# A short store of zeros into the output, issued beside the first load of a streaming softmax

## The chip, the cores and the metric

One core of one Trainium2 chip runs the kernel. The metric is the time of one execution on the device in microseconds (us), lower is better. Nine executions of the kernel before, taken in one series, lie between 317.75 and 318.42 us (0.2%), so an effect of half a microsecond in 318 needs several runs and the trace to be seen.

## The reference

A softmax over the last axis with a temperature of 0.5; the input is 32 x 512 rows of 1024 float32 values, 64 MB in and 64 MB out.

```python
def reference(x, temperature):
    scaled = x / temperature
    shifted = scaled - np.max(scaled, axis=-1, keepdims=True)
    exp_x = np.exp(shifted)
    return (exp_x / np.sum(exp_x, axis=-1, keepdims=True)).astype(np.float32)
```

## The kernel before

Sixteen tiles of 4 MB (128 partitions x 8 rows of 1024) stream through six buffers. SyncE (SP) issues the loads and ScalarE (ACT) the stores. VectorE (DVE) takes maxima over groups of four rows and divides; ScalarE exponentiates. Each partition's 8 rows lie next to each other in memory, so a load or a store is 128 pieces of 32 KB.

```python
TILES = [[8]] * 16
BUFS = 6
GROUP = 4
# ... pools, groups, dram() cut
    def load():
        i = len(tiles)
        if i < len(TILES):
            xt = data.tile([P, sum(TILES[i]), d], f32, name="xt")
            nc.sync.dma_start(out=xt, in_=dram(xf, i))                   # L61
            tiles.append(xt)
# ... maximum, exponential, divide cut: L70, L79, L91 and L93 of the profile
    def store(g):
        i, _, _, part = groups[g]
        if part:
            a, k = part
            nc.scalar.dma_start(out=dram(of, i)[:, a : a + k, :],
                                in_=tiles[i][:, a : a + k, :])           # L101
            if a + k == sum(TILES[i]):
                load()

    with tc.manual_schedule():
        for _ in range(BUFS):
            load()
        for g in range(len(groups) + 1):
            if g < len(groups):
                maximum(g)
                exponential(g)
            if g > 0:
                divide(g - 1)
                store(g - 1)
```

Of the kernel before, what the change touches and what calls it, by code (L numbers as in the profile page):

```python
# [1 line left out]

# [4 lines left out]
# [9 lines that stand above are left out]
@with_exitstack  # L16
def kernel(
    ctx: ExitStack,
    tc: tile.TileContext,
    x: bass.AP,  # L20
    temperature: bass.AP,
    out: bass.AP,
):
    nc = tc.nc
    f32 = mybir.dt.float32
    scale = 1.0 / float(temperature)
    extreme = mybir.AluOpType.max if scale > 0 else mybir.AluOpType.min

    P = 128
    xf = x.flatten_outer_dims()  # L30
    of = out.flatten_outer_dims()
    n, d = xf.shape
    assert sum(sum(ks) for ks in TILES) * P == n

    data = ctx.enter_context(tc.tile_pool(name="data", bufs=BUFS))
    stats = ctx.enter_context(tc.tile_pool(name="stats", bufs=4))


    groups, first, r = [], [], 0
    for i, ks in enumerate(TILES):  # L40
        first.append(r)
        r += sum(ks)
        a = 0
        for k in ks:
            for b in range(0, k, GROUP):
                m = min(GROUP, k - b)
                groups.append((i, a + b, m, (a, k) if b + m == k else None))
            a += k

    def dram(t, i):  # L50
        k = sum(TILES[i])
        block = t[P * first[i] : P * (first[i] + k), :]
        return block.rearrange("(p k) d -> p k d", p=P, k=k)

    tiles, small = [], []
# [8 lines that stand above are left out]
    def maximum(g):  # L64
        i, a, k, _ = groups[g]
        top, bias, sums, recip = (
            stats.tile([P, k], f32, name=name) for name in ("top", "bias", "sums", "recip")
        )
        small.append((bias, sums, recip))
        nc.vector.tensor_reduce(  # L70
            out=top, in_=tiles[i][:, a : a + k, :], axis=mybir.AxisListType.X, op=extreme
        )
        nc.vector.tensor_scalar_mul(bias, in0=top, scalar1=-scale)  # L73

    def exponential(g):
        i, a, k, _ = groups[g]
        bias, sums, _ = small[g]
        for b in range(k):
            nc.scalar.activation(  # L79
                tiles[i][:, a + b, :],  # L80
                tiles[i][:, a + b, :],
                mybir.ActivationFunctionType.Exp,
                bias=bias[:, b : b + 1],
                scale=scale,
                accum_out=sums[:, b : b + 1],
            )

    def divide(g):
        i, a, k, _ = groups[g]
        _, sums, recip = small[g]  # L90
        nc.vector.reciprocal(recip, sums)  # L91
        for b in range(k):
            nc.vector.tensor_scalar_mul(  # L93
                tiles[i][:, a + b, :], in0=tiles[i][:, a + b, :], scalar1=recip[:, b : b + 1]
# [6 lines that stand above are left out]
            nc.scalar.dma_start(out=dram(of, i)[:, a : a + k, :], in_=tiles[i][:, a : a + k, :])  # L101
            if a + k == sum(TILES[i]):
                load()



    with tc.manual_schedule():
        for _ in range(BUFS):
            load()
        for g in range(len(groups) + 1):  # L110
# [8 lines that stand above are left out]
# [1 line left out]
_INS = ['x', 'temperature']  # L120
_OUTS = [((32, 512, 1024), 'float32')]

_NUMBERS = {'temperature': 0.5}


# [26 lines left out]
```

## Time and profile before

| before | |
|---|---|
| time, median of 3 runs | 317.91 us (317.78 to 318.01) |
| span of the profiled run | 316.0 us |
| data packets | 4096 of 32 KB, 256 per DMA engine, median 1.213 us each: 310.5 us |
| first data packet starts / last packet ends | 1.74 us / 314.80 us |
| VectorE busy | 75% |

The packet rows come from the trace's record of every DMA packet (start, duration, bytes, queue). Sixteen engines at 32768 bytes per 1.213 us make 432 GB/s. From 1.74 us to the end they hardly ever stop, so the kernel is bound by DMA, and any microsecond that all engines lose should reach the end.

From the profile page of the kernel before: busy times, the DMA row over 40 slices of 7.9 us (9 is 90% or more busy), the two queues (q1 is SyncE's, with the loads; q10 is ScalarE's, with the stores: packets, MB, share of 16 engines), and the chain of work that ended last.

```profile
span 316.0 us, 620 instructions
...
DVE 235.5 (75%) x224; ACT 149.6 (47%) x257; POOL 0.2 (0%) x4
...
DMA  8999999999999999999999999999999999999996
...
DMA packets 4612, 134.25 MB, mean 425 GB/s; under 512 B 512, under 2 KB 512, under 8 KB 512
...
q1 hardware_dynamic: 2304, 67.11, 49.7%
q10 hardware_dynamic: 2304, 67.11, 49.2%
...
DVE 49%; DMA 32%; another core or an unknown queue 9%; ACT 5%; issue 1%; DVEq 0%; SPq 0%
```

The reader should see the nines in the DMA row and the shares of the queues: 49.7% and 49.2% add up to 99%. The chain names VectorE for half of the span, but it is no steady measure: it names VectorE for 49% here and for 72% in the trace of the memset alone (below), which runs equally fast. An engine that is busy 75% does not bound a kernel whose DMA engines are busy 99%.

From the timeline of the kernel before, its start and its last stores (start, duration, both in us, engine, line, operation; in brackets, how long the engine had been idle and what released it). "SPq" and "ACTq" are DMA issues, x6 means six merged.

```profile
0.73 2.91 SPq L61 DMA_DIRECT2D xt<-in_x_dram  x6
12.96 4.42 DVE L70 TENSOR_REDUCE top<-xt 128x4 f32<-128x4096 f32 x1 [12.96 <-DMA xt<-in_x_dram]
13.01 1.28 ACT L79 ACT_TABLE_LOAD   x1 [13.01 <-DMA xt<-in_x_dram]
...
32.66 0.37 ACTq L101 DMA_DIRECT2D out_dram<-xt  x1
...
302.38 0.34 ACTq L101 DMA_DIRECT2D out_dram<-xt  x1
```

VectorE and ScalarE idle for 13 us, the first store is issued at 32.66 us and the last at 302.38.

Beyond the 310.5 us, the packet records hold two groups of load packets that take longer than 1.213 us. I call "stretch" the sum of what the load packets took beyond 1.213 us, divided by 16 engines:

```
kernel before, load packets over 1.26 us          packets   durations          stretch per engine
1.74 to 2.10 us   (first packet of each engine)        16    1.66 to 2.06 us    0.69 us
33.93 to 35.92 us (after the first store's issue)      28    1.27 to 2.60 us    0.81 us
rest of the kernel                                      4    1.48 to 1.75 us    0.14 us with smaller ones
```

The second group begins 1.27 us after the first store is issued. This group is what the change could hope to remove. In the table of windows (DVE, ACT, POOL busy, TensorE clock, DMA share, GB/s) it shows only coarsely, because a window of 4 us holds about three packets per engine and each is counted at once:

```profile
30.00:33.00 3.00, 3.00 (x5) 3.00 (x5) 0.00 (x0) 1.00 1.14 492
33.00:37.00 4.00, 3.97 (x2) 1.45 (x4) 0.00 (x0) 1.00 0.87 287
```

### The profile page before, as it was taken

To read this page: it belongs to the slowest core of one execution; us is meant where nothing else is said; L and a number is where in the kernel's file an instruction comes from. 1 tells how busy PE (TensorE), PEld (TensorE's weight loads), DVE (VectorE), ACT (ScalarE), POOL (GpSimd) and SP (SyncE) were. 2 spreads that over 40 slices of the span, in tenths; PEclk is the share of its full clock that TensorE was granted. 3 is DMA by queue.
4 is the path that set the end of the run, shared out by engine and by line. 5 is a ranking of instruction groups with operands and counts; after the bars stand their busy time and mean duration, and the time that the engine had idled before them with its cause. 6 is when DMAs were issued, how large, how long until landed. Compare 5 with 4: busy or idle time off the path is not lost.

```text
span 316.0 us, 620 instructions
## 1 busy us (share of the span) xinstructions
DVE 235.5 (75%) x224; ACT 149.6 (47%) x257; POOL 0.2 (0%) x4
## 2 busy tenths in 40 slices
DVE  0399999999689494994949859497693976949720
ACT  0176666666526255361554605546064560645500
POOL 0000000000000000000000000000000000000000
DMA  8999999999999999999999999999999999999996
GB/s 332 411 452 423 373 460 415 452 425 431 436 427 440 427 444 423 444 419 448 415 452 411 452 408 456 423 444 427 436 431 432 440 423 444 419 444 419 452 411 274
DMA packets 4612, 134.25 MB, mean 425 GB/s; under 512 B 512, under 2 KB 512, under 8 KB 512
## 3 DMA queue, kind: packets, MB, share of 16 engines
q1 hardware_dynamic: 2304, 67.11, 49.7%
q10 hardware_dynamic: 2304, 67.11, 49.2%
q14 instruction: 4, 0.03, 0.0%
HBM read 67.11 MB, written 67.11 MB: 425 GB/s over the span
## 4 chain that ended last, share of the span: by engine, by line
DVE 49%; DMA 32%; another core or an unknown queue 9%; ACT 5%; issue 1%; DVEq 0%; SPq 0%
DVE top L70 29%; DMA xt<-in_x_dram 20%; DVE xt L93 18%; DMA out_dram<-xt 12%; ACT xt L79 5%; DVE recip L91 1%; DVE bias L73 1%; DVEq L147 0%; SPq L61 0%
## 5 line engine op out<-in xcount | busy, mean ns | idle before, releaser
L79 ACT ACTIVATE xt<-xt,bias 128x1024 f32<-128x1024 f32 x128 | 145.4, 1137 | 136.8 <-DVE recip L91 119.4
L70 DVE TENSOR_REDUCE top<-xt 128x4 f32<-128x4096 f32 x32 | 141.3, 4416 | 62.6 <-DMA xt<-in_x_dram 62.6
L93 DVE TENSOR_SCALAR xt<-xt,recip 128x1024 f32<-128x1024 f32 x128 | 87.7, 749 | 1.1
L79 ACT ACTIVATION_READ_ACCUMULATOR xt<-xt,bias 128x1 f32 x128 | 23.9, 187 | 0.0
L79 ACT ACT_TABLE_LOAD x1 | 1.3, 1283 | 13.0 <-DMA xt<-in_x_dram 13.0
L91 DVE RECIPROCAL recip<-sums 128x4 f32<-128x4 f32 x32 | 5.5, 171 | 2.1 <-ACT xt L79 2.1
L73 DVE TENSOR_SCALAR bias<-top 128x4 f32<-128x4 f32 x32 | 5.4, 170 | 1.1
L133 POOL MEMSET const-bfloat16-1.0<- 128x1 bf16 x1 | 0.1, 101 | 0.0
L133 POOL MEMSET const-uint8-127<- 128x1 uint8 x1 | 0.1, 101 | 0.0
L133 POOL MEMSET const-float32-0.0<- 128x1 f32 x1 | 0.1, 98 | 0.2 <-issue 0.2
L133 POOL MEMSET const-float32-1.0<- 128x1 f32 x1 | 0.1, 98 | 0.0
## 6 DMA issues: line engine op xcount, KB each, us to landing
xt<-in_x_dram SPq DMA_DIRECT2D x16, 4096.0 KB, 50.2
out_dram<-xt ACTq DMA_DIRECT2D x16, 4096.0 KB, 38.6
```

The costliest lines, as they stand in the source:

```text
L70: nc.vector.tensor_reduce(out=top, in_=tiles[i][:, a : a + k, :], axis=mybir.AxisListType.X, op=extreme)
L73: nc.vector.tensor_scalar_mul(bias, in0=top, scalar1=-scale)
L79: nc.scalar.activation(tiles[i][:, a + b, :], tiles[i][:, a + b, :], mybir.ActivationFunctionType.Exp, bias=bias[:, b : b + 1], scale=scal ...
L91: nc.vector.reciprocal(recip, sums)
L93: nc.vector.tensor_scalar_mul(tiles[i][:, a + b, :], in0=tiles[i][:, a + b, :], scalar1=recip[:, b : b + 1])
L133: nc = _bacc.Bacc("TRN2", target_bir_lowering=False, num_devices=1)
```

## The change

A tile of 128 x 128 zeros is cleared on VectorE and stored from ScalarE's queue into the first 512 bytes of each partition's share of the first output tile, before anything else. The first tile's real store overwrites it. The likely intent is to use the store queue and the output once while nothing depends on them.

```diff
+    zeros = stats.tile([P, 128], f32, name="zeros", bufs=1)
     with tc.manual_schedule():
+        nc.vector.memset(zeros, 0.0)
+        nc.scalar.dma_start(out=dram(of, 0)[:, 0, :128], in_=zeros)
         for _ in range(BUFS):
             load()
```

## The prediction

> **What bounds the kernel now.** The DMA engines. The page's DMA row is 9 in 38 of 40 slices, 425 GB/s over the span, for 134 MB. The trace's records of single DMA packets say it more sharply: 4096 data packets of 32 KB, 256 on each of 16 engines, median 1.213 us. That is 432 GB/s in all, close to the 435.2 GB/s fabric ceiling that the Trainium skill gives (DMA: Bandwidth & Descriptors, section "Where 436 GB/s comes from"). 256 x 1.213 = 310.6 us of the 316.0 us span. The first packet starts at 1.74 us, the last one ends at 314.8; over these 313.1 us the engines lie idle 1.6 us on average, nearly all in the last microsecond. VectorE is busy 75% and waits 62.6 us for loads (list of waits); it does not bound the whole.
>
> The rest above 310.6 us is a few stretched packets, in two clusters. (1) The first packet on each engine takes 1.66 to 2.06 us: about 0.7 us lost once. (2) Right after the first store is issued (32.66 us), two load packets in a row on each engine stretch, to about 1.5 and 1.8 us: about 0.8 us lost by all 16 engines, once. No later store shows it. In the table of windows, 33 to 37 us moves 287 GB/s (coarse: a packet is counted at once).
>
> **What the change does.** Adds a memset of 128x128 on VectorE (estimated 0.1 to 0.2 us, from 0.75 us for a 128x1024 operation), while VectorE waits for the first load until 12.96 us anyway: free. Adds one DMA issue on ScalarE's queue (0.34 us, as the others there), also in idle time. Adds 128 packets of 512 B, 64 KB: 0.15 us at 432 GB/s; with per-packet overhead I estimate 0.2 to 0.4 us, partly inside the latency of the first load's packets. The order of instructions shows that DMA semaphores shift by one: the sixth load now waits for the first load (13 us), which costs nothing, as four loads are still queued then; the first tile's store waits for the zeros, landed about 28 us before. All else keeps its order.
>
> **What it may gain.** ScalarE's queue and the output are now used first at about 1 to 2 us. If cluster (2) is a cost of first use of that queue (or of the first write), it is paid there, overlapping cluster (1), and the 0.8 us at 34 to 37 us go. All DMA time is on the critical path: load 15 lands at 281 us, computing it ends just as store 14 drains, and store 15 follows without a gap; an early gain reaches the end whole. Net: -0.8 x 0.7 (my trust in the mechanism) + 0.2 = about -0.4 us, rounded to -0.5.
>
> **Prediction.** 317.4 us, 8 in 10 between 316.9 and 318.3. Chances: faster by over 2% 0.01, within 2% 0.97, slower by over 2% 0.02. A gain of 2%, 6.4 us, is more than all idle and stretched time found.
>
> **What would show it.** The zeros' packets between 1.5 and 4 us; no packet over 1.3 us between 33 and 37 us; the first load landing at most 0.4 us later than now (12.2 us after its issue); later loads landing and the last store issued about 0.5 us earlier.
>
> **What would make it wrong.** The stretched packets come from the first large store itself (its descriptors, or the turn from reading to writing under load), and stay: then 318.1 us. Or the two slow starts add up: 318.0. Or short writes cost far more than their bytes.

## The result

| | before | after |
|---|---|---|
| time, median of 6 runs | 318.01 us (317.78 to 318.39) | 318.46 us (318.18 to 319.06) |
| ratio | | 1.0017 (95%: 1.0004 to 1.003) |
| span of the profiled run | 315.99 us | 316.40 us |
| last DMA packet ends | 314.80 us | 315.00 us |
| from there to the end of the span | 1.19 us | 1.41 us |
| stretch after the first real store | 0.81 us | 0.70 us |

Ratios are the mean time of one kernel's fast runs over that of the other's of the same rounds, so they are not quite the ratio of the medians. By the medians the kernel became slower by about half a microsecond (the interval of the ratio allows 0.1 to 1.0), where I had predicted it faster by as much; 318.46 lies above the range that ended at 318.3.

From the profile page after; the chain is now told as mostly DMA, which says nothing new, as the chain is unsteady (see above):

```profile
span 316.4 us, 623 instructions
...
DVE 235.6 (74%) x225; ACT 149.6 (47%) x257; POOL 0.2 (0%) x4
...
DMA  8999999999999999999999999999999999999995
...
DMA packets 4756, 134.32 MB, mean 425 GB/s; under 512 B 528, under 2 KB 656, under 8 KB 656
...
q1 hardware_dynamic: 2304, 67.11, 49.6%
q10 hardware_dynamic: 2448, 67.18, 49.2%
...
DMA 57%; DVE 26%; ACT 6%; another core or an unknown queue 4%; issue 1%; DVEq 0%; SPq 0%
```

The store queue has 144 packets more: 128 of zeros and 16 that signal completion. From the timeline after:

```profile
0.73 12.70 SPq L61 DMA_DIRECT2D xt<-in_x_dram  x6
0.82 0.17 DVE L111 MEMSET zeros<- 128x128 f32 x1 [0.82 <-PEq L138]
1.02 0.41 ACTq L112 DMA_DIRECT2D out_dram<-zeros  x1
13.11 4.42 DVE L70 TENSOR_REDUCE top<-xt 128x4 f32<-128x4096 f32 x1 [12.12 <-DMA xt<-in_x_dram]
13.16 1.28 ACT L79 ACT_TABLE_LOAD   x1 [13.16 <-DMA xt<-in_x_dram]
...
32.81 0.34 ACTq L101 DMA_DIRECT2D out_dram<-xt  x1
...
302.54 0.34 ACTq L101 DMA_DIRECT2D out_dram<-xt  x1
```

The memset takes 0.17 us and delays nothing. The six load issues now stretch over 12.70 us instead of 2.91, because the sixth waits for the first load; that is the shift of semaphores foreseen. It costs nothing: the sixth load's last packet ends at 86.57 us (86.44 before). In this pair of traces VectorE starts 0.15 us later, the first and the last real store are issued 0.15 and 0.16 us later, and the last packet ends 0.20 us later. That looks like one early delay carried to the end, but single traces scatter as much: with the memset alone (below) VectorE starts at 12.94 us, yet the last store is issued 0.12 us later than before and the last packet ends at 314.94 us. What an early packet costs at the end is measured by the eightfold store below.

From the list of DMA issues after (KB each, median us from issue to landing):

```profile
out_dram<-zeros ACTq DMA_DIRECT2D x1, 64.0 KB, 14.5
```

64 KB needed 14.5 us to land. The packet records show why. On one engine, in the kernel after:

```
start us   duration   bytes   queue
 6.088      27 ns       512   q10 (zeros)
 6.111    1213 ns     32768   q1  (load)
 7.321      27 ns       512   q10
 7.344    1213 ns     32768   q1
 8.553      27 ns       512   q10
```

The engine takes one packet from each queue in turn. That is what the Trainium skill says (DMA: Bandwidth & Descriptors, section "Queues, rings and completion order": each engine goes round the queue rows it has work for, packet by packet), and the trace agrees, if one record of it is taken as a packet: 8 packets of zeros per engine lie between 6.09 and 14.02 us, one per load packet. Each costs the engine 27 ns, so the store costs every engine 8 x 27 ns = 0.22 us. The turns do not explain why the first packet starts only 5.07 us after the issue at 1.02 us, for a turn lasts 1.24 us. The first real store behaves likewise: issued at 32.81 us, its first packet starts at 37.20 us. What fills this time is not shown.

From the same windows after:

```profile
30.00:33.00 3.00, 2.97 (x5) 3.00 (x5) 0.00 (x0) 1.00 0.91 393
33.00:37.00 4.00, 4.00 (x1) 1.59 (x4) 0.00 (x0) 1.00 1.01 360
```

One might read 360 against 287 GB/s as a gain. It is not: the window before it lost as much, as packets moved across the edge. The records of single packets show load packets stretched from 34.12 us on, 1.31 us after the first real store's issue, by 0.70 us per engine in all. The zeros did not remove them.

The last 0.2 us come after all data has landed. The records of the queue instructions at the end of the program, which no view lists, show ScalarE late at its last DRAIN (the trace's name for an instruction with which each engine closes the program):

```
last DRAIN of            SyncE starts    ScalarE starts, takes     span ends
before                     315.56          315.57      8 ns         315.99
after                      315.77          316.05    136 ns         316.40
```

Each engine's last record follows only after all have been at this point (ScalarE's starts at 315.93 us before, 316.34 after). Before, ScalarE is there with SyncE; after, 0.28 us later.

So the theory was: 0.22 us for the zeros' packets, about 0.2 us for a late end of ScalarE's instruction stream, and no gain, because the stretch does not come from first use of the queue or of the output.

### The profile page after: what moved, and what is told of

The parts are those of the page before. It is cut to its first block, busy times and chain, and to the rows that moved or that the text cites. A ratio compares the mean times of both kernels' runs of the same rounds, so it can differ in the third digit from the quotient of the medians.

```text
span 316.4 us, 623 instructions
## 1 busy us (share of the span) xinstructions
DVE 235.6 (74%) x225; ACT 149.6 (47%) x257; POOL 0.2 (0%) x4
## 4 chain that ended last, share of the span: by engine, by line
DMA 57%; DVE 26%; ACT 6%; another core or an unknown queue 4%; issue 1%; DVEq 0%; SPq 0%
DMA xt<-in_x_dram 35%; DMA out_dram<-xt 22%; DVE top L70 17%; DVE xt L93 9%; ACT xt L79 6%; DVE recip L91 1%; DVE bias L73 0%; DVEq L152 0%; SPq L61 0%
## 6 DMA issues: line engine op xcount, KB each, us to landing
out_dram<-zeros ACTq DMA_DIRECT2D x1, 64.0 KB, 14.5
```

## The experiments

"Stretch" is as above, over the 6 us after the issue named. "Tail" is the time from the last packet's end to the end of the span. All runs were correct. Those with five rounds are compared with runs of the kernel before on the same chip.

### The change once more

No edit.

> The change itself once more, for its size on the same chip as the three below. Theory A (the zeros' own packets cost the DMA engines 8 x 27 ns each, about 0.2 us, and the ScalarE instruction stream, one DMA longer, loses another 0.2 us in the teardown after the last packet, as in the first trace, where ScalarE's last DRAIN came 0.28 us after the other engines' and took 136 ns): 0.3 to 0.6 us slower than before. Theory B (the second three of the six runs, 319.0, were only scatter, and the real cost is the packets alone): 0.1 to 0.3 us slower. In the trace: stretched load packets at 34 to 37 us again, summing to 0.7 to 0.8 us per engine.

Measured: 318.45 us against 317.94, ratio 1.0013 (1.0 to 1.0025), tail 1.38 us, ScalarE's last DRAIN 0.29 us behind SyncE's and 136 ns long; stretch after the first real store 0.52 us. The slowdown of half a microsecond is there again, though the interval begins at 1.0; the two runs at 319.0 of the first series did not come again and are taken as scatter. The stretch fell below the 0.7 expected, but it is there, on 19 packets.

### The memset alone

```diff
-        nc.scalar.dma_start(out=dram(of, 0)[:, 0, :128], in_=zeros)
```

> The memset stays, the store goes. Both theories: equal to before within 0.1 us, for the memset runs while VectorE waits for the first load. If it is slower by 0.2 us or more, the cost is not in the DMA at all. Stretched packets at 34 to 37 us as before.

Measured: 317.98 against 317.94, ratio 1.0 (0.9987 to 1.0012), tail 1.19 us, stretch 0.94 us. The memset is free. Over the traces in which the first real store is issued near 33 us (leaving out that with the early 16-partition store), the stretch is 0.70 to 0.94 us in the six without zeros on ScalarE's queue and 0.52 to 0.75 us in the four with them. A saving of about 0.1 us by the zeros can't be told from scatter, nor excluded; one of the whole 0.8 us is excluded.

### The zeros on the other queue

```diff
-        nc.scalar.dma_start(out=dram(of, 0)[:, 0, :128], in_=zeros)
-        for _ in range(BUFS):
+        load()
+        nc.sync.dma_start(out=dram(of, 0)[:, 0, :128], in_=zeros)
+        for _ in range(BUFS - 1):
             load()
```

> The same zeros store, but issued on SyncE's queue right after the first load; ScalarE's instruction stream and queue are as before. Theory A: 0.1 to 0.3 us slower than before (packets only), and in the trace 0.75 us instead of 0.95 us between the last store's landing seen by SyncE and the end of the span. If the cost comes from the use of ScalarE's queue as such: no cost. The zeros land near 13 us, right behind the first load. The stretch at 34 to 37 us stays at 0.7 to 0.8 us, as ScalarE's queue is now used first by the first real store.

Measured: 318.22 against 317.94, ratio 1.0005 (0.9993 to 1.0018), tail 1.21 us, no late DRAIN, stretch 0.80 us. From the list of DMA issues:

```profile
out_dram<-zeros SPq DMA_DIRECT2D x1, 64.0 KB, 12.1
```

The medians differ by 0.28 us, as expected for the packets alone, though the interval includes zero. The tail is back at its old value, and that is read from the trace, not from the times.

### The store eight times as large

```diff
-    zeros = stats.tile([P, 128], f32, name="zeros", bufs=1)
+    zeros = stats.tile([P, 1024], f32, name="zeros", bufs=1)
-        nc.scalar.dma_start(out=dram(of, 0)[:, 0, :128], in_=zeros)
+        nc.scalar.dma_start(out=dram(of, 0)[:, 0, :], in_=zeros)
```

> The store is 8 times as large (4 KB per partition, 512 KB in all), the same 8 packets per engine. If early DMA time reaches the end one for one: 8 x 4 KB at 27 GB/s is 1.21 us per engine, so 1.2 to 1.7 us slower than before. If the change's cost is a fixed one (an extra DMA, a longer stream, a shifted semaphore): 0.4 to 0.6 us slower, as the change itself. If a larger early store primes what the first real store stretches on, the stretch at 34 to 37 us shrinks below 0.4 us per engine and the time is 0.4 us lower than that.

Measured: 319.31 against 317.94, ratio 1.0041 (1.0027 to 1.0055), so 1.37 us slower. The zeros' 8 packets per engine took 159 ns each, 1.27 us together, against 0.22 us in the change: 1.05 us more, and the kernel is 0.86 us slower than the change in the medians and 1.21 us in the spans. So DMA time lost in the first microseconds reached the end about one for one. The tail is 1.41 us, the stretch 0.75 us: a larger early store does not remove it either.

### The last store moved off ScalarE's queue

On top of the change:

```diff
-            nc.scalar.dma_start(out=dram(of, i)[:, a : a + k, :], ...)
+            queue = nc.sync if i == len(TILES) - 1 else nc.scalar
+            queue.dma_start(out=dram(of, i)[:, a : a + k, :], ...)
```

> The change, with the last tile's store issued from SyncE instead of ScalarE: ScalarE has again 16 DMA issues, as before the change, while the zeros stay on ScalarE's queue. Theory S (ScalarE's longer instruction stream, 321 recorded instructions against 319 and 320, makes its last DRAIN late): from the last packet's end to the end of the span about 1.2 us as before, not 1.4; time 0.1 to 0.3 us above before, about 0.2 below the change. Theory Q (having used ScalarE's queue for a short store is what costs in the teardown): 1.4 us, 0.4 to 0.5 above before.

Measured: 318.09 against 317.94, ratio 1.0009 (0.9995 to 1.0023), tail 1.21 us, no late DRAIN. The zeros are still stored from ScalarE, but ScalarE's stream is down to 320 recorded instructions and the 0.2 us are gone. Use of the queue is not the reason for the tail.

### ScalarE's stream made longer without any store

Kernel before, with two or with 24 tiny copies:

```diff
+    tiny = stats.tile([P, 2], f32, name="tiny", bufs=1)
     with tc.manual_schedule():
+        nc.vector.memset(tiny, 0.0)
+        for _ in range(2):      # 24 in the other kernel
+            nc.scalar.copy(out=tiny[:, 1:2], in_=tiny[:, 0:1])
```

> The kernel before, with no store of zeros, but two tiny copies (128x1) ahead of ScalarE's work, so that its stream is as long as the change's. Theory S: 1.4 us from the last packet to the end, ScalarE's last DRAIN of 136 ns 0.2 to 0.3 us behind the other engines', and 0.15 to 0.25 us slower than before, with no extra DMA at all. Theory Q: 1.2 us and equal to before within 0.1 us.

> The same with 24 tiny copies (about 5 us of ScalarE's idle time before 13 us). If Theory S is about where the end of ScalarE's stream falls (a fixed spot in it where an instruction comes late), 24 instructions more move that spot away from the end, into time in which ScalarE waits: 1.2 us from the last packet to the end, equal to before within 0.1 us. If any longer stream is slower: 1.4 us, 0.15 to 0.25 us slower, as with two.

Measured with two copies: 318.15 against 317.94, ratio 1.001 (0.9997 to 1.0022), tail 1.39 us, ScalarE's last DRAIN 0.27 us late and 135 ns long. With 24: 318.10, ratio 1.0009 (0.9996 to 1.0021), tail 1.17 us, no late DRAIN; its five times scatter from 317.79 to 318.56, so the expectation of equal times within 0.1 us was not met, while that of the tail was. Put together, from the traces:

```
recorded ScalarE instructions   kernels                                      last DRAIN late   tail
319                             before, memset alone,                        no                1.19, 1.19,
                                the three with a store held back (below)                       1.15, 1.16, 1.19
320                             zeros on the other queue, last store moved,  no                1.21, 1.21, 1.20
                                the early 16-partition store (below)
321                             the change (twice), 8 times as large,        0.27 to 0.29 us   1.41, 1.38, 1.41,
                                two tiny copies                                                1.39
322                             the early whole-tile store (below)           no                1.30
343                             24 tiny copies                               no                1.17
```

The late end goes with one length of the stream and not with the zeros. Two tiny copies, without any extra DMA, produce it.

The DMA records hold a sign of why. The queue of instructions (q14) carries 8 KB packets, and three of them move when ScalarE's stream grows: with 24 copies they start at 49.23, 162.32 and 279.08 us, for about 65.0, 181.93 and 316.96 us before. The third lies near the end of the program in most kernels: 1.03 to 1.41 us after ScalarE's last DRAIN starts where the stream has 319 or 320 instructions, 0.65 to 0.93 us after it where it has 321, and before it where it has 322 (at 325.62 us, DRAIN at 332.98) or 343. So the late DRAIN stands next to a fetch of instructions. That the fetch delays it is not shown.

### When does the stretch come: the second store held back

Kernel before; the second tile's store is issued with the third's, so that the store queue runs empty for a while.

```diff
+                if g - 1 == 3:
+                    continue
+                if g - 1 == 5:
+                    store(3)
                 store(g - 1)
```

> The kernel before, with the second tile's store held back and issued together with the third's (near 62 us instead of 47), so that ScalarE's queue runs empty from about 56 to 62 us while loads go on. Theory R (load packets stretch whenever 32 KB store packets join after the store queue was empty): a second group of stretched load packets from about 63 to 67 us, again 0.5 to 0.9 us per engine, beside the one at 34 to 37 us. Theory F (it is paid once, by the first large store of the kernel): no more than the 0.1 to 0.2 us that the records already show there beside an instruction fetch at 65 us.

Measured, one run: 322.84 us. The first store was issued at 32.63 us, with a stretch of 0.80 us. The next issue found the queue without data packets since 54.48 us:

```profile
59.90 0.34 ACTq L101 DMA_DIRECT2D out_dram<-xt  x1
...
62.19 0.34 ACTq L101 DMA_DIRECT2D out_dram<-xt  x1
```

Up to 65 us no load packet stretched at all; two did then, beside an instruction fetch, as in the kernel before. These stores joined again after a pause and did not pay; the theory that they must falls, on one run. The 4.9 us that this kernel lost came later (see the last section).

### The first store later

Kernel before; in the first kernel the first tile's store is held back until the second's, in the other by half a tile.

```diff
+                if g - 1 == 1:
+                    continue
+                if g - 1 == 3:      # 2 in the other kernel
+                    store(1)
                 store(g - 1)
```

> The kernel before, with the first tile's store held back and issued with the second's, near 47.4 us. Theory F: the stretched load packets move with the issue, to about 48.5 to 52 us, 0.5 us or more, none at 33 to 37.5 us. Theory P: none at 33 to 37.5 us, and little (under 0.3 us) at 48.5 to 52 us, as the load then stands in the middle of its tile. Theory T (something else at this time, not the store): 0.7 us stays at 33 to 37.5 us.

> The same with the first store one half-tile later (near 40 us instead of 32.7). Theory F: stretch of 0.5 us or more from about 41 to 45 us. Theory P: under 0.3 us there, and then perhaps 0.3 to 0.7 us faster than before, unless the later start of the stores costs as in the run with the second store held back.

Measured: 318.27 us (one run) and 318.72 us against 318.01, ratio 1.0033 (1.0011 to 1.0054). From the timeline with the store held until the second's, and of the half-tile kernel in the second block:

```profile
44.93 0.37 ACTq L101 DMA_DIRECT2D out_dram<-xt  x1
...
47.52 0.34 ACTq L101 DMA_DIRECT2D out_dram<-xt  x1
```

```profile
37.19 0.37 ACTq L101 DMA_DIRECT2D out_dram<-xt  x1
...
47.41 0.34 ACTq L101 DMA_DIRECT2D out_dram<-xt  x1
```

Both issues came earlier than I had said (44.9 for 47.4, 37.2 for 40), as a held store waits for nothing. The stretched load packets came from 46.17 us (0.76 us per engine) and from 38.80 us (1.02 us); neither kernel shows any between 33 us and its own first store. So the stretch follows the first store, wherever the load then stands in its tile, and holding it back gains nothing.

### One early store of full-size packets, 16 partitions

Kernel before:

```diff
                 exponential(g)
+                if g == 0:
+                    nc.scalar.dma_start(out=dram(of, len(TILES) - 1)[0:16],
+                                        in_=tiles[1][0:16])
```

> The kernel before, with one early store of full-size packets: 16 partitions x 32 KB of the second tile, raw, to rows that the last tile's store overwrites, issued from ScalarE near 22.3 us, one packet per engine. Theory F (the stretch of 0.7 to 0.8 us is paid once, by the first store with large packets): the stretched load packets move to about 23.5 to 27 us, and 33 to 37.5 us shows under 0.2 us; time 1.2 us (the 16 extra packets) above before. Theory P (the stretch comes from where in its tile a load stands when the first whole-tile store joins, whatever was stored before): 0.5 us or more stays at 33 to 37.5 us.

Measured: 333.74 us median, the four runs from 326.86 to 343.2. Three are slow, the profiled one (333.9) among them, so the time is not used. In the one profiled run no load packet stretched in the 6 us after the early issue at 22.72 us, nor after the first real store at 33.23. But the 16 early packets themselves took 3.0 to 4.1 us each, 2.5 us per engine beyond 1.213. This fits Theory F only in that the first real store paid nothing, although the early one was no whole tile but had pieces of 32 KB; the cost did not appear in load packets, as I had expected. Because this store has another shape than a full tile's, and the trace is of a slow run, I tried a cleaner form.

### One early store as large as a real one

On top of the change, with a buffer less to make room:

```diff
-BUFS = 6
+BUFS = 5
-    zeros = stats.tile([P, 128], f32, name="zeros", bufs=1)
+    zeros = stats.tile([P, 8192], f32, name="zeros", bufs=1)
-        nc.scalar.dma_start(out=dram(of, 0)[:, 0, :128], in_=zeros)
+        nc.scalar.dma_start(out=dram(of, 0), in_=zeros.rearrange("p (k d) -> p k d", k=8))
```

> The change with the early store of zeros as large as a real store: the whole first tile, 128 packets of 32 KB, with 5 tile buffers instead of 6 to make room for the zeros. Theory F (the first store whose packets are as large as the real ones pays the stretch once): load packets stretch by 0.5 us or more per engine in the 4 us after the zeros are issued (at about 5 to 10 us), and 33 to 37.5 us shows under 0.2 us. If the stretch belongs to the first store of computed tiles whatever came before: 0.5 us or more at 33 to 37.5 us again. The time means nothing here beyond the extra 4 MB, which alone are 9.7 us at 432 GB/s.

Measured, one run: 335.18 us, which means nothing beyond the 4 MB more and the buffer less. From its timeline:

```profile
2.50 6.88 DVE L111 MEMSET zeros<- 128x8192 f32 x1 [2.50 <-issue]
...
9.42 0.37 ACTq L112 DMA_DIRECT2D out_dram<-zeros  x1
...
33.41 4.42 DVE L70 TENSOR_REDUCE top<-xt 128x4 f32<-128x4096 f32 x1 [7.93 <-DMA xt<-in_x_dram]
...
40.92 0.34 ACTq L101 DMA_DIRECT2D out_dram<-xt  x1
```

Load packets stretched from 10.90 to 12.83 us, after the issue of the zeros, by 0.71 us per engine. After the first real store, at 40.92 us (later than I had assumed: VectorE waited until 33.41 us for the second load, and the store follows its divide), the stretch was 0.00. This run tells most, though it is one run: the first store of 32 KB pieces pays about 0.7 us once, zeros or not, and the next one does not. The short store does not count as such a store; one of 4 KB per partition does not either.

One rival is not separated: "first" may mean the first on this queue instead of the first of the kernel. The kernel with the last store moved bears on it. That store, issued at 302.63 us, is the 16th of a whole tile but the first on SyncE's queue, and 13 of its own packets took 1.34 to 2.23 us, 0.41 us per engine in all. With the last store on ScalarE's queue, no packet after its issue exceeded 1.26 us, in twelve traces of thirteen (in that of the whole-tile zeros two did, up to 1.52 us). No run here stores whole tiles on both queues early, so this stays open.

## Why the prediction was wrong

**The step that failed** is "If cluster (2) is a cost of first use of that queue (or of the first write), it is paid there, overlapping cluster (1), and the 0.8 us at 34 to 37 us go". The queue and the output were used early, and most or all of the 0.8 us stayed: 0.70 and 0.52 us with the change, 0.75 us with the eightfold store, against 0.81 before and 0.94 us with the memset alone. The runs put in its place that the cost belongs to the first store of 32 KB pieces (of the kernel or of the queue): it moved with that store to 38.8 and 46.2 us, did not come back after the store queue had run empty, and was paid by the zeros, at 11 to 13 us, only when these were as large as a tile. Such a store costs 9.7 us of DMA time at 432 GB/s (128 x 32 KB), so nothing can be won by it. I had named this outcome as the first thing that would make me wrong ("The stretched packets come from the first large store itself"), and gave it 0.3 against 0.7.

**The cost of the zeros** I had at 0.2 to 0.4 us of engine time. It was 0.22 us, and it lay inside no latency: the packets went out one by one between load packets already moving at full rate. The first load landed 0.15 us later, within my 0.4.

**When the zeros would move** I had wrong: 6.09 to 14.02 us instead of 1.5 to 4. The length comes from the packet-by-packet turn between the queues, of which I did not think; the late start, 5.07 us after the issue, is not explained by it and stays open.

**What I had not seen** is the tail: 0.2 us after the last packet, from ScalarE's stream having grown from 319 to 321 instructions. My "stay" case was 318.1; with 0.2 us more it would have been 318.3, and the median of 318.46 came with a median of 318.01 for the kernel before. The sum of the two costs, 0.22 + 0.2, agrees with the measured 0.45 and 0.51 us. By their times alone, the kernels with one cost each (0.28, 0.15 and 0.21 us) are not clear of zero. The traces show the tail clearly. They do not show the 0.22 us at the end of the program: without zeros or a store held back the last packet ended at 314.80 to 315.56 us, with the short zeros at 315.00 to 315.32 us. For that part the eightfold store stands.

**What held:** the kernel is bound by DMA (1.05 us of early packets cost 0.86 to 1.21 us at the end), the memset and the waits by shifted semaphores are free, and the change is far within 2%. (The 1.6 us of idle engines in the prediction is 0.85 us by the data packets' records, 313.06 less 312.21; nothing rests on it.)

**What stays open:** why the first store of 32 KB pieces slows the loads before its own first packet starts (33.93 to 35.92 against 37.13 us), and why packets of 512 bytes or 4 KB do not bring this about; and why a stream of 321 instructions ends late. For the latter the Trainium skill offers a candidate (Runtime: NRT & Kernel Launch, section "Instruction fetch mechanics": instructions are refilled in blocks of 256, and crossing a block costs little). The trace agrees in part: 8 KB instruction packets come 127 recorded ScalarE instructions apart (after the 67th and the 194th in the kernel before), so closer than the page says, and one lies 0.65 to 0.93 us after each late DRAIN. That it causes the delay is only argued.

No version here beats the kernel before.

## What to carry to other kernels

A short transfer did not "warm up" the DMA queue for large ones here: see which transfer the slow packets follow, by moving it, before spending an instruction on it. In this kernel, bound by DMA, packets added at the start were paid at the end (1.05 us of them cost 0.86 to 1.21). A short store beside a queue of large packets landed late (14.5 us after its issue), since it started late and then got one turn per large packet. When half a microsecond is at stake, look also at what happens after the last byte has landed; two instructions more on an idle engine can cost as much as the transfer they issue.

## What the Trainium skill lacked or had wrong

- DMA: Bandwidth & Descriptors has no figure for a small packet of SyncE's or ScalarE's queue beside bulk traffic. Here a 512-byte packet took 27 ns and one of 4 KB took 159 ns of its engine, against 1.213 us for 32 KB; the 64 KB store started 5.07 us and landed 14.5 us after its issue beside a load queue with 32 KB packets, though it cost the engines 0.22 us.
- The same page does not tell that the first store of 32 KB pieces slows the loads beside it once, nearly all before its own packets start: 0.5 to 1.0 us per engine beginning 1.0 to 1.6 us after its issue, in every kernel here but the one with the early 16-partition store.
- No page tells that the relative position of the load and store streams can matter. With the second store held back, loads and stores changed tiles about 2.4 us apart (the seventh load's first packet at 80.70 us, the third store's at 83.12), against 7.8 us before (the sixth load's at 68.02, the third store's at 75.86), and 3.9 us per engine of stretched packets came after 37.5 us, against 0.16 us before; the time was 322.84 us. The kernel with the early 16-partition store looks alike: sixth load at 73.68 us, third store at 75.78, 2.1 us apart, 5.9 us per engine of stretched packets after 37.5 us, profiled time 333.9 us. One trace of each, and the cause is not shown.
- Runtime: NRT & Kernel Launch, "Instruction fetch mechanics", calls the cost of crossing an instruction block mostly hidden. If the late DRAIN is such a crossing, which is not shown, 0.2 us of it is not hidden at the end of a program. The page gives refills of 256 instructions; here the instruction packets are of 8 KB and come 127 recorded ScalarE instructions apart.
